# Stick-breaking groups 4 to 6: score matmuls over each head's 64 rows, one split of q for two heads, high parts on ScalarE, the scan's carry read in place

## The chip, the cores and the metric

The kernel runs on one core of one Trainium2 chip. The metric is device time in microseconds (us), the median of several executions. The core has TensorE (PE, with its weight loads as PEld), VectorE (DVE), ScalarE (ACT), GpSimd (POOL) and SyncE (SP, which here issues nearly all DMAs). Each engine works through its own queue in order; engines wait for each other by semaphores.

## The reference

One transformer layer over 2048 tokens of width 1024: a normed projection, differential attention (4 heads) beside stick-breaking attention (8 heads of 64), an output projection and a SwiGLU feed-forward part. What the change touches is the stick-breaking part:

```python
def stick_breaking_attention(q, k, v):
    """A[t,s] = beta_ts * prod_{s<j<t}(1 - beta_tj), s < t."""
    ...
        z = jnp.einsum('bqhd,bkhd->bhqk', qb, k).astype(jnp.float32) * scale
        mask = (k_pos[None, :] < q_pos[:, None])[None, None]
        log_1mb = jnp.where(mask, jax.nn.log_sigmoid(-z), 0.0)
        rem = lax.cumsum(log_1mb, axis=3, reverse=True) - log_1mb
        a = jnp.where(mask, jnp.exp(jax.nn.log_sigmoid(z) + rem), 0.0)
        return jnp.einsum('bhqk,bkhd->bqhd', a.astype(v.dtype), v)
```

Each weight is a sigmoid of the score times the product of (1 - sigmoid) over all later keys up to the query, so the keys are gone through backwards with a running product.

## The kernel before

**Stages.** The first part goes through eight groups: 0 to 3 are the heads of differential attention, 4 to 7 are pairs of stick-breaking heads (a group is m = 0 and m = 1). While group g does its attention, the projections of group g + 1 are made, tile by tile (16 tiles of 128 tokens); `advance` interleaves the two. Then come the output projection and the feed-forward part. The order of instructions on each engine is made by a scheduler that runs a timeline of its own, with the priorities `PRI`; it starts from the order of the program text. `pick` shares work between engines by a running sum of assumed costs in `load`, `note` adds to that sum, and `level` sets it back.

**Precision.** Every f32 operand of a matmul is split in a high and a low f16 part, and three products (high x high, low x high, high x low) are added up in PSUM. The high part is a scaled copy, made on ACT or DVE; the low part is made on DVE from the source and the high part (`split_psum`).

**Projections of groups 4 to 6 ("turned").** `proj_turned` makes q and k already transposed: PSUM tile `pq` has the 64 dimensions of head 0 in partitions 0 to 63 and those of head 1 in partitions 64 to 127, and two tokens' tiles side by side. `turned_out` (L345) takes a pair of tiles, 256 columns, out of PSUM. In `qT` it writes four slots: for each head m a high part and a low part, with `half[:, m]` as the scale, which is 2^-11 on the head's own 64 partitions and 0 on the others. k has one high and one low part for both heads. Group 7 is not turned; it goes through `proj_tile`, `proj_out` and `proj_batch` as the differential groups do.

**Scores.** `score_chunk` (L503) makes the scores of 128 queries against up to 512 keys in one PSUM tile `sc`, of which there are four. For turned groups it multiplies all 128 partitions of a `qT` slot with all 128 of `kT`; the zeros in q take the other head out. At the last chunk of a row of scores one more matmul (L508) adds the mask.

**Stage a** (`stage_a`, L602) goes through a block of up to 1024 keys of one query tile and one head, from the last chunk to the first. `z4` tiles (nine buffers) hold `om` and `be`. ACT makes 1 - beta into `om` and beta into `sc` or `be`. DVE's scan (L621) turns `om` into running products, backwards. Its start value and the neighbour that the multiply needs stand in the column behind the block, `om[:, n]`:

```python
if b == i // 8:
    DVE.memset(om[:, n : n + 1], 8192.0)
else:
    DVE.tensor_copy(om[:, n : n + 1], last[m][:, 0:1])
```

Then beta is multiplied with the products, shifted by one column (L622): on POOL for the second chunk of a turned group (`aside`), else on DVE. `split_t` splits the result (high part on ACT, low part by a subtraction on POOL, L98) and a transposing DMA (L460) brings it to `aT`. A group has 48 such stages.

**Stage b** multiplies `aT` with v on PE (`pv`, L517) some stages later (`lag`); `finish` norms the result.

Of the kernel before, what the change touches and what calls it, by code (L numbers as in the profile page):

```python
# [16 lines left out]
ALU = mybir.AluOpType  # L17
# [4 lines left out]
S, D, P = 2048, 1024, 128  # L22
# [37 lines left out]
def block(tc, a, out):  # L60
# [3 lines left out]
    with top:  # L64
# [8 lines left out]
        def note(e, ns):  # L73
            load[e] += ns * KW[e]
# [38 lines left out]
        def c1(n=1, name="c"):  # L113
            t = cp.tile([P, n], F32, name=nm(name))
            return t
# [10 lines left out]
        mhalf = c1(16, "mh")  # L126
        DVE.memset(mhalf[:], -0.5)

        half = c1(2, "half")
        DVE.memset(half[:], 0.0)  # L130
        for m in range(2):
            DVE.memset(half[64 * m : 64 * m + 64, m : m + 1], 2.0 ** -11)

        def times(o, a_, b_, c=None):
            DVE.tensor_scalar(o[:], a_[:], b_[:], c, op0=ALU.mult, **({} if c is None else {"op1": ALU.mult}))
# [120 lines left out]
        with ExitStack() as ph1:  # L256
# [87 lines left out]
            @pri("po")  # L344
            def turned_out(pq, pv, qT, kT, v, j):  # L345
                two = slice(j - 1, j + 1)
                q2, k2 = (pq[:, 256 * c : 256 * c + 256].rearrange("p (t n) -> p t n", t=2) for c in range(2))
                for m in range(2):
                    ACT.mul(qT[:, m, two, :], q2, half[:, m : m + 1])
                    DVE.scalar_tensor_tensor(qT[:, 2 + m, two, :], q2, half[:, m : m + 1], qT[:, m, two, :], op0=ALU.mult, op1=ALU.subtract)  # L350
                note("A", 800)
                note("D", 800)
                split_psum(kT[:, 0, two, :], kT[:, 1, two, :], k2, 256)
                vv = v[:, two, :].rearrange("p t (h s e) -> p t h s e", h=2, s=2)
                split_psum(vv[:, :, :, 0, :], vv[:, :, :, 1, :], pv[:, :256].rearrange("p (t h e) -> p t h e", t=2, h=2), 256)

            def split_psum(hi, lo, src, n):
                sc = 2.0 ** -11
                if pick(A=0.84 * n + 60, D=1.05 * n + 70) == "A":
                    ACT.mul(hi, src, sc)  # L360
                else:
                    DVE.tensor_scalar(hi, src, sc, None, op0=ALU.mult)
                DVE.scalar_tensor_tensor(lo, src, sc, hi, op0=ALU.mult, op1=ALU.subtract)  # L363
                note("D", 1.05 * n + 70)
# [136 lines left out]

            @pri("sc")
            def score_chunk(G, sc, i, q, m, w, cut=False, turned=False):  # L503
                terms = ((m, 0), (2 + m, 0), (m, 1)) if turned else ((2 + m, m), (m, m))
                for o, (a_, b_) in enumerate(terms):
                    last = PE.matmul(sc[:, : 128 * w].rearrange("p (t n) -> p t n", n=P), lhsT=G["q"][i // 4][:, a_, i % 4, :], rhs=G["k"][q][:, b_, 0:w, :], start=o == 0, stop=o == len(terms) - 1)  # L506
                if cut:
                    last = PE.matmul(sc[:, 128 * w - P : 128 * w], lhsT=idb[:], rhs=tri[:], start=False, stop=True, skip_group_check=True)  # L508
                return last.ins
# [85 lines left out]
            def sb_attn(g, G):  # L595
                last = {}
                front = []
                wide = [0]
                lag = PD + 2 if g < NG - 2 else PD

                @pri("at")
                def stage_a(i, m, b):  # L602
                    L = (i + 1) * 128
                    n = min(1024, L - 1024 * b)
                    be, om = z4(), z4()
                    if b == i // 8:
                        DVE.memset(om[:, n : n + 1], 8192.0)
                    else:
                        DVE.tensor_copy(om[:, n : n + 1], last[m][:, 0:1])
                    last[m] = om  # L610
                    for c in range((n - 1) // 512, -1, -1):
                        lo, hi = 512 * c, min(512 * c + 512, n)
                        w = hi - lo
                        sc = ps.tile([P, 512], F32, tag="sc", bufs=4, name=nm("sc"))
                        front.append(score_chunk(G, sc, i, 2 * b + c, m, w // P, b == i // 8 and hi == n, turned(g)))
                        aside = c == 1 and turned(g)
                        beta = be[:, lo:hi] if aside else sc[:, :w]
                        ACT.activation(om[:, lo:hi], sc[:, :w], AF.Sigmoid, scale=G["nkz"][:])  # L618
                        ACT.activation(beta, sc[:, :w], AF.Sigmoid, scale=G["kz"][:])  # L619
                        ov = om[:, lo:hi][:, ::-1]  # L620
                        DVE.tensor_tensor_scan(ov, ov, sc[:, :w], om[:, hi : hi + 1], op0=ALU.mult, op1=ALU.bypass)  # L621
                        (POOL if aside else DVE).tensor_tensor(be[:, lo:hi], beta, om[:, lo + 1 : hi + 1], ALU.mult)  # L622
# [24 lines left out]
                for i in range(NT):  # L647
                    if i % 4 == 0:
                        level()
                    for b in range(i // 8, -1, -1):  # L650
                        for m in range(2):
                            n, aT = stage_a(i, m, b)
                            pend.append((i, m, b, n, aT))
                            if len(pend) > lag:
                                stage_b(*pend.pop(0))
                            done += n // P + CS
                            yield done / (272 + 48 * CS), (i + 1 if b == 0 and m == 1 else i)
                for u in pend:
                    stage_b(*u)
# [213 lines left out]
        with ExitStack() as ph2:  # L873
# [21 lines left out]
            rows = []  # L895
# [402 lines left out]
```

## Time and profile before

| | |
|---|---|
| median of 3 runs | 2706.24 us (2704.32 to 2712.25) |
| the profiled execution | 2704.82 us |
| its span, first to last instruction | 2702.7 us |
| mean granted TensorE clock | 0.983 |
| busy share PE, DVE, ACT, POOL | 93%, 72%, 50%, 56% |
| scans (L621) | from 602.2 us, the last from 1349.9 us |

The span is what the views of the profile divide. Busy times of PE are too long as a measure of need, since matmuls overlap in the pipeline. The views by stretches give the busy time of each engine between two times; the groups by shape give a line's instructions, their count, busy time, mean length in ns, and the engine's idle time before them with what ended it.

### The profile page before, as it was taken

The numbers are of one execution on the slowest core, as the hardware profiler recorded it, in microseconds if no ns is written. First come the engines' busy times: TensorE is split into PE (matmuls) and PEld (weight loads), VectorE is DVE, ScalarE is ACT, GpSimd is POOL, SyncE is SP. The second block draws the span as 40 slices with busy tenths as digits, with TensorE's granted clock in tenths as the row PEclk, the third lists the DMA queues.
The fourth block names the chain that finished last, engine by engine and source line by source line (L and its number), as shares of the span: only waits on it lengthen the run. The fifth ranks groups of instructions, "written<-read, shape, count | busy, mean of one in ns | idle before, by whom it ended". The sixth has DMA issues, their size and how long they took to land. (4 is left out here: it accounts for less than half of the span.)

```text
span 2702.7 us, 50511 instructions
## 1 busy us (share of the span) xinstructions
PE 2500.8 (93%) x19628; PEld 1502.5 (56%) x19628; DVE 1956.5 (72%) x3711; ACT 1346.4 (50%) x2488; POOL 1516.4 (56%) x1097
## 2 busy tenths in 40 slices
PE   7998989898988989889998999999999999999999
PEld 4655556577776776567784444444444444444444
DVE  6888879899989989877856777778685543433434
ACT  4665656567978878665735534345352112111121
POOL 2577767767767767546655565565564332322322
PEclk9999999999999999999999999999999999999999
DMA  7777687769989989987995566565749744635532
GB/s 230 201 166 180 143 200 173 178 151 178 196 176 185 178 169 209 206 200 211 222 335 204 210 236 220 198 234 190 253 171 338 293 158 160 234 132 184 201 111 94
DMA packets 619584, 534.40 MB, mean 198 GB/s; under 512 B 480640, under 2 KB 548224, under 8 KB 609104
## 3 DMA queue, kind: packets, MB, share of 16 engines
q1 hardware_dynamic: 617520, 529.09, 69.8%
q8 instruction: 154, 2.52, 0.4%
q0 software_dynamic: 512, 1.36, 0.2%
q10 hardware_dynamic: 1312, 0.72, 0.1%
q14 instruction: 86, 0.70, 0.1%
HBM read 261.08 MB, written 147.32 MB: 151 GB/s over the span
## 5 line engine op out<-in xcount | busy, mean ns | idle before, releaser
L98 POOL TENSOR_TENSOR s<-z,s 128x1024 f16<-128x1024 f32 (+7 forms) x288 | 471.9, 1648 | 140.9 <-ACT s L89 116.3
L506 PE MATMUL sc<-kT,qT 128*128 128x512 f16 (+3 forms) x1520 | 381.6, 353 | 53.5 <-DVE z L622 19.0
L1104 PE MATMUL pd<-wd,act 128*128 128x512 f16 x1764 | 391.8, 379 | 8.1 <-DVE cu L1038 7.1
L621 DVE TENSOR_TENSOR_SCAN z<-z,sc 128x512 f32<-128x512 f32 (+3 forms) x320 | 352.8, 1112 | 56.7 <-ACT sc L619 34.9
L325 PE MATMUL pj<-w,xt 128*128 128x384 f16 x1920 | 353.1, 332 | 17.2 <-ACT raw L374 5.9
L1004 PEld LDWEIGHTS <-wg 128*128 128x128 f16 x1848 | 181.5, 98 | 226.1 <-issue 12.4
L1004 PEld LDWEIGHTS <-wu 128*128 128x128 f16 x1848 | 181.5, 98 | 220.2 <-issue 7.1
L517 PE MATMUL yp<-v,aT 128*128 128x64 f16 (+1 forms) x4896 | 269.1, 204 | 37.3 <-DMA aT<-s 36.2
L517 PEld LDWEIGHTS <-aT 128*128 128x128 f16 x4896 | 236.9, 99 | 115.4 <-DMA aT<-s 47.7
L98 POOL TENSOR_TENSOR act<-cg,act 128x512 f16<-128x512 f32 x109 | 150.6, 1392 | 262.5 <-ACT act L1063 262.5
L1104 PEld LDWEIGHTS <-act 128*128 128x128 f16 x1764 | 172.6, 98 | 216.6 <-issue 10.1
L325 PEld LDWEIGHTS <-xt 128*128 128x128 f16 x1920 | 187.5, 99 | 146.9 <-issue 23.3
L89 ACT CAST s<-z 128x128 f16<-128x128 f32 (+7 forms) x215 | 173.1, 810 | 135.8 <-DMA aT<-s 41.0
L98 POOL TENSOR_TENSOR stages<-stages 128x512 f32<-128x512 f32 x97 | 171.6, 1769 | 119.1 <-DVE wg L220 41.3
L618 ACT ACTIVATE z<-sc,c 128x512 f32<-128x512 f32 (+3 forms) x320 | 210.6, 663 | 25.1 <-PE sc L506 12.5
L98 POOL TENSOR_TENSOR hs<-hs,cu 128x512 f32<-128x512 f32 x102 | 132.5, 1307 | 158.1 <-DVE hs L1110 58.0
L506 PEld LDWEIGHTS <-qT 128*128 128x128 f16 x1520 | 128.2, 99 | 121.4 <-issue 23.5
L1063 ACT CAST act<-cg 128x512 f16<-128x512 f32 x126 | 76.8, 616 | 237.5 <-DVE cg L1069 199.4
L831 PE MATMUL po<-wo,mt 128*128 128x256 f16 x1536 | 182.5, 279 | 12.2 <-DVE xf L834 8.4
L1110 DVE SCALAR_TENSOR_TENSOR hs<-pd,c,hs 128x512 f32<-128x512 f32 x144 | 106.5, 748 | 116.3 <-PE pd L1104 112.2
L341 PE MATMUL pj<-xt,w 128*128 128x128 f16 x2304 | 176.9, 222 | 6.2 <-DVE v L363 5.2
L1004 PE MATMUL pm<-X,wu 128*128 128x512 f16 x792 | 179.3, 379 | 1.8 <-ACT cg L1049 1.7
(255 smaller groups left out, 4803.5 us busy)
## 6 DMA issues: line engine op xcount, KB each, us to landing
xt<-xs SPq DMA_DIRECT2D x112, 512.0 KB, 4.3
hs<-hd SPq DMA_DIRECT2D x72, 512.0 KB, 4.4
hd<-hs SPq DMA_DIRECT2D x56, 512.0 KB, 5.4
split<-wg SPq DMA_DIRECT2D x11, 1792.0 KB, 6.9
split<-wu SPq DMA_DIRECT2D x11, 1792.0 KB, 6.7
split<-wd SPq DMA_DIRECT2D x11, 1792.0 KB, 6.8
wg<-split SPq DMA_DIRECT2D x11, 1792.0 KB, 7.3
wd<-split SPq DMA_DIRECT2D x11, 1792.0 KB, 8.7
```

Of the source, the lines that this page charges most:

```text
L89: ACT.copy(dst, src)
L98: (DVE if e == "D" else POOL).tensor_tensor(dst, a_, b_, op)
L325: PE.matmul(pj[:, :384], lhsT=xv[:, xi, kt, :], rhs=G["w"][:, wi, kt, :], start=n == 0, stop=n == 23)
L341: PE.matmul(o, lhsT=x_ if c == 2 else w_, rhs=w_ if c == 2 else x_, start=n == 0, stop=n == 23)
L506: last = PE.matmul(sc[:, : 128 * w].rearrange("p (t n) -> p t n", n=P), lhsT=G["q"][i // 4][:, a_, i % 4, :], rhs=G["k"][q][:, b_, 0:w, :] ...
L517: PE.matmul(yp[:, y0 : y0 + wd], lhsT=aT[:, a_, :], rhs=v[:, v_ : v_ + wd], start=start and j == 0 and q == 0, stop=stop and j == nb - 1 a ...
L618: ACT.activation(om[:, lo:hi], sc[:, :w], AF.Sigmoid, scale=G["nkz"][:])
L621: DVE.tensor_tensor_scan(ov, ov, sc[:, :w], om[:, hi : hi + 1], op0=ALU.mult, op1=ALU.bypass)
L831: PE.matmul(po[:, sl], lhsT=mt[:, kt, P * xi : P * xi + P], rhs=wos[2 * h + n][wi][:, kt, :], start=q == 0, stop=q == 23)
L1004: PE.matmul(ps_[:].rearrange("p (t n) -> p t n", n=P), lhsT=wv[:, wo, wi, 128 * kt : 128 * kt + 128], rhs=X[xo][:, :, xi, kt, :], start=st ...
L1104: PE.matmul(po[:], lhsT=act[:, ao, xi, 128 * j : 128 * j + 128], rhs=W["d"][:, wo, wi, :], start=start and u == 0 and q == 0, stop=u == nu ...
L1110: DVE.scalar_tensor_tensor(dst, po[:], kd[:], src, op0=ALU.mult, op1=ALU.add)
```

## The change

Four things change, all of them in the stick-breaking groups.

- `turned_out` makes one high and one low part of q for both heads, in slots 0 and 1 of `qT`, by `split_psum`; the tile `half` is gone, and so are the two `note` lines. All three high parts (q, k, v) of the turned groups are made on ACT (`he="A"`); the low parts stay on DVE.
- `score_chunk` takes for turned groups the 64 partitions of head m from q and from k, instead of all 128. The number of matmuls and their columns stay, as do the other matmuls.
- The column behind the block, `om[:, n]`, is written by POOL, not by DVE, in all four stick-breaking groups.
- The scan's start value is read from where it comes from: a constant tile `full`, the first column of the block done before (`last[m]`), or the first column of the chunk done before. The multiply at L622 still reads the column.

```diff
-        half = c1(2, "half")
-        DVE.memset(half[:], 0.0)
-        for m in range(2):
-            DVE.memset(half[64 * m : 64 * m + 64, m : m + 1], 2.0 ** -11)
+        full = c1(1, "full")
+        DVE.memset(full[:], 8192.0)
...
             def turned_out(pq, pv, qT, kT, v, j):
...
-                for m in range(2):
-                    ACT.mul(qT[:, m, two, :], q2, half[:, m : m + 1])
-                    DVE.scalar_tensor_tensor(qT[:, 2 + m, two, :], q2, half[:, m : m + 1], qT[:, m, two, :], op0=ALU.mult, op1=ALU.subtract)
-                note("A", 800)
-                note("D", 800)
-                split_psum(kT[:, 0, two, :], kT[:, 1, two, :], k2, 256)
+                split_psum(qT[:, 0, two, :], qT[:, 1, two, :], q2, 256, "A")
+                split_psum(kT[:, 0, two, :], kT[:, 1, two, :], k2, 256, "A")
                 vv = v[:, two, :].rearrange("p t (h s e) -> p t h s e", h=2, s=2)
-                split_psum(vv[:, :, :, 0, :], vv[:, :, :, 1, :], pv[:, :256].rearrange(...), 256)
+                split_psum(vv[:, :, :, 0, :], vv[:, :, :, 1, :], pv[:, :256].rearrange(...), 256, "A")
-            def split_psum(hi, lo, src, n):
+            def split_psum(hi, lo, src, n, he="AD"):
                 sc = 2.0 ** -11
-                if pick(A=0.84 * n + 60, D=1.05 * n + 70) == "A":
+                cost = {"A": 0.84 * n + 60, "D": 1.05 * n + 70}
+                if pick(**{e: cost[e] for e in he}) == "A":
...
             def score_chunk(G, sc, i, q, m, w, cut=False, turned=False):
-                terms = ((m, 0), (2 + m, 0), (m, 1)) if turned else ((2 + m, m), (m, m))
+                rows = slice(64 * m, 64 * m + 64) if turned else slice(0, P)
+                terms = ((0, 0), (1, 0), (0, 1)) if turned else ((2 + m, m), (m, m))
                 for o, (a_, b_) in enumerate(terms):
-                    ... lhsT=G["q"][i // 4][:, a_, i % 4, :], rhs=G["k"][q][:, b_, 0:w, :] ...
+                    ... lhsT=G["q"][i // 4][rows, a_, i % 4, :], rhs=G["k"][q][rows, b_, 0:w, :] ...
...
                     if b == i // 8:
-                        DVE.memset(om[:, n : n + 1], 8192.0)
+                        begin = full[:]
+                        POOL.memset(om[:, n : n + 1], 8192.0)
                     else:
-                        DVE.tensor_copy(om[:, n : n + 1], last[m][:, 0:1])
+                        begin = last[m][:, 0:1]
+                        POOL.tensor_scalar(om[:, n : n + 1], begin, 1.0, 0.0, op0=ALU.mult, op1=ALU.add)
...
-                        DVE.tensor_tensor_scan(ov, ov, sc[:, :w], om[:, hi : hi + 1], op0=ALU.mult, op1=ALU.bypass)
+                        DVE.tensor_tensor_scan(ov, ov, sc[:, :w], begin, op0=ALU.mult, op1=ALU.bypass)
+                        begin = om[:, lo : lo + 1]
```

More of the change, by code (lines that the diff above doesn't have):

```diff
@@ L503, in score_chunk @@
             def score_chunk(G, sc, i, q, m, w, cut=False, turned=False):
-                terms = ((m, 0), (2 + m, 0), (m, 1)) if turned else ((2 + m, m), (m, m))
+                rows = slice(64 * m, 64 * m + 64) if turned else slice(0, P)
+                terms = ((0, 0), (1, 0), (0, 1)) if turned else ((2 + m, m), (m, m))
                 for o, (a_, b_) in enumerate(terms):
-                    last = PE.matmul(sc[:, : 128 * w].rearrange("p (t n) -> p t n", n=P), lhsT=G["q"][i // 4][:, a_, i % 4, :], rhs=G["k"][q][:, b_, 0:w, :], start=o == 0, stop=o == len(terms) - 1)
+                    last = PE.matmul(sc[:, : 128 * w].rearrange("p (t n) -> p t n", n=P), lhsT=G["q"][i // 4][rows, a_, i % 4, :], rhs=G["k"][q][rows, b_, 0:w, :], start=o == 0, stop=o == len(terms) - 1)
                 if cut:
```

2 lines of the change are left out of this document (1 added, 1 removed).

## The prediction

> **What bounds the kernel now.** I read the page first for the span, then the view by stretches for the stick-breaking part, then the groups by shape inside that part, then the waits of the score matmuls.
>
> ```profile
> span 2702.7 us, 50511 instructions
> PE 2500.8 (93%) x19628; PEld 1502.5 (56%) x19628; DVE 1956.5 (72%) x3711; ACT 1346.4 (50%) x2488; POOL 1516.4 (56%) x1097
> ```
>
> The average says "TensorE", but the change touches one part only: groups 4 to 7, which last from the first scan at 602 us to the last at 1351. The scans come 80 to a group; the 1st, 81st, 161st and 241st begin at 602, 762, 921 and 1092 us, and these are the stretches (busy us of PE, PEld, DVE, ACT, POOL; granted clock; DMA share; GB/s).
>
> ```profile
> core 0: us, PE busy (x) PEld busy (x) DVE busy (x) ACT busy (x) POOL busy (x), PEclk, DMA share, GB/s
> 602.00:762.00 160.00, 145.90 (x2227) 118.37 (x2224) 148.18 (x256) 138.93 (x259) 123.26 (x92) 0.98 0.94 185
> 762.00:921.00 159.00, 142.26 (x2260) 114.85 (x2258) 144.99 (x252) 132.73 (x242) 117.21 (x89) 1.00 0.95 185
> 921.00:1092.00 171.00, 152.31 (x2071) 114.66 (x2066) 150.26 (x266) 131.37 (x238) 116.96 (x89) 0.97 0.92 187
> 1092.00:1351.00 259.00, 228.12 (x2367) 178.09 (x2366) 204.68 (x356) 165.78 (x305) 146.37 (x101) 0.96 0.86 209
> ```
>
> Groups 4 to 6 take 490 us. In them DVE works 148.18 + 144.99 + 150.26 = 443 us, ACT 403, POOL 357. PE's 440 us overstate it, since a matmul's record holds its pipeline as well. What PE really needs is the count of each shape times the distance between starts when nothing is waited for. The distances come from an undisturbed piece of the timeline (start, length, how many):
>
> ```profile
> 840.62 0.82 PE L506 MATMUL sc<-kT,qT 128*128 128x512 f16 x3 [0.62 <-DVE z L622]
> 841.27 0.57 PE L517 MATMUL yp<-v,aT 128*128 128x64 f16 x14
> 841.68 0.64 PE L488 MATMUL yp<-id,y 128*128 128x128 f32 x4
> 842.15 0.46 PE L517 MATMUL yp<-v,aT 128*128 128x64 f16 x10
> 851.24 2.24 PE L341 MATMUL pj<-xt,w 128*128 128x128 f16 x37
> ```
>
> Three score matmuls over 512 columns fill 841.27 - 840.62 = 0.65 us, 0.217 each; fourteen over 64 columns 0.41 us, 0.029 each; thirty-seven over 128 columns 2.24 us less one pipeline of 0.2, 0.056 each. It goes by columns. The counts from 602 to 1092 us:
>
> ```profile
> L341 PE MATMUL pj<-xt,w 128*128 128x128 f16 x2016 | 154.1, 222 | 6.1 <-DVE v L363 5.2 <-POOL z L622 0.9
> L506 PE MATMUL sc<-kT,qT 128*128 128x512 f16 x504 | 138.8, 386 | 21.7 <-DVE z L622 10.7 <-DVE z L609 4.0 <-DVE z L621 3.4
> L517 PE MATMUL yp<-v,aT 128*128 128x64 f16 x2352 | 105.0, 194 | 10.1 <-DMA aT<-s 10.0
> L341 PE MATMUL pj<-w,xt 128*128 128x128 f16 x1008 | 90.0, 219 | 0.0
> L325 PE MATMUL pj<-w,xt 128*128 128x384 f16 x168 | 29.1, 326 | 0.3 <-DVE v L363 0.3
> L508 PE MATMUL sc<-tri,idb 128*128 128x128 bf16 x97 | 21.3, 221 | 0.0
> L506 PE MATMUL sc<-kT,qT 128*128 128x384 f16 x72 | 16.3, 326 | 1.5 <-DVE z L607 1.4
> L506 PE MATMUL sc<-kT,qT 128*128 128x256 f16 x74 | 12.7, 280 | 1.4 <-DVE z L622 1.0 <-DVE z L621 0.3
> L517 PE MATMUL yp<-v,aT 128*128 128x128 f16 x130 | 9.5, 224 | 0.4 <-DMA aT<-s 0.4
> L506 PE MATMUL sc<-kT,qT 128*128 128x128 f16 x70 | 8.6, 223 | 2.1 <-DVE z L607 1.0 <-DVE z L621 0.4 <-DVE z L622 0.3
> ```
>
> At 0.217, 0.165, 0.110, 0.056 and 0.029 us for 512, 384, 256, 128 and 64 columns: projections 3024 x 0.056 + 168 x 0.165 = 197; scores 504 x 0.217 + 72 x 0.165 + 74 x 0.110 + 70 x 0.056 = 133; values 2352 x 0.029 + 130 x 0.056 = 75; cuts 97 x 0.056 = 5; with some 60 small ones at about 0.12 (7 us) PE needs 418 us of 490. So DVE is the tallest (443, 47 us idle), PE second (418, 72 idle), ACT third. And PE, when it stands at a score matmul, mostly waits for DVE (us, times, 602 to 1092):
>
> ```profile
>   DVE z L622: 25.7, 33
>   DVE z L607: 9.3, 16
>   DVE z L609: 8.8, 14
>   DVE z L621: 4.0, 11
> ```
>
> 48 of PE's 72 idle us are these: a score buffer that DVE gives back late.
>
> **DVE's part of the change (a gain).** Rows of 540 to 1092 us for the splits, of the whole run for the carry column:
>
> ```profile
> L350 DVE SCALAR_TENSOR_TENSOR qT<-pj,half,qT 128x256 f16<-128x256 f32 x48 | 22.7, 473 | 2.4 <-ACT qT L349 2.3
> L362 DVE TENSOR_SCALAR kT<-pj 128x256 f16<-128x256 f32 x20 | 8.2, 412 | 0.0
> L362 DVE TENSOR_SCALAR v<-pj 128x256 f16<-128x256 f32 x15 | 6.1, 408 | 0.6 <-PE pj L341 0.5
> L609 DVE COPY z<-z 128x1 f32<-128x1 f32 x64 | 8.2, 143 | 0.0
> L607 DVE MEMSET z<- 128x1 f32 x128 | 7.2, 59 | 0.3 <-POOL s L98 0.3
> ```
>
> Half of the low q parts go: 24 x 0.473 = 11.3 us. All high k and v parts leave DVE: 8.2 + 6.1 = 14.3. The carry column leaves it: 15.4, three quarters of it in groups 4 to 6 (11.6), a quarter in group 7 (3.8). In groups 4 to 6 that is 37 us, a little of it before 602: say 35, and DVE falls from 443 to 408.
>
> **ACT's part (even).**
>
> ```profile
> L349 ACT ACTIVATE qT<-pj,half 128x256 f16<-128x256 f32 x48 | 24.6, 513 | 21.6 <-PE pj L341 15.2 <-DVE qT L350 6.3
> L360 ACT ACTIVATE v<-pj 128x256 f16<-128x256 f32 x9 | 4.0, 442 | 1.6 <-PE pj L341 1.6
> L360 ACT ACTIVATE kT<-pj 128x256 f16<-128x256 f32 x4 | 1.5, 386 | 0.6 <-DVE qT L350 0.6
> ```
>
> 48 q parts at 0.513 (24.6 us) become 24 at about 0.386 (9.3), and 20 k parts and 15 v parts come over at 0.386 and 0.442 (14.4): 24.6 out, 23.7 in. ACT stays at 402.
>
> **POOL's part (a cost beside the path).** The carry column's 128 fills and 64 copies go to POOL. The nearest rows are its one-column fills at the start and its smallest arithmetic, over four columns (ns: least, median, most):
>
> ```profile
> L1284 POOL MEMSET const-float32-0.0<- x1: 100/100/100, 0.2 to 0.2; 128x1 f32 x1
> L484 POOL TENSOR_SCALAR yrs<-yrs x16: 233/242/1212, 136.7 to 631.4; 128x4 f32<-128x4 f32 x16
> ```
>
> 96 x 0.10 + 48 x 0.24 = 21 us in groups 4 to 6: POOL goes from 357 to 379, still the lowest. The scan now reads its carry from the old place and waits for no column, but the multiply behind the first chunk still reads the column, so it now waits for POOL.
>
> **PE's part (a cost).** The number of score matmuls and their columns stays. What changes is that they work on 64 rows of the array, among projections, values and cuts on 128. The kernel before has one such case, the bias matmuls on 32 rows, and the last of them lies at full clock:
>
> ```profile
> 32.97 0.49 PE L325 MATMUL pj<-w,xt 128*128 128x384 f16 x2
> 33.38 0.91 PE L703 MATMUL bt<-z,z 32*128 32x384 f32 x2
> 34.22 0.66 PE L325 MATMUL pj<-w,xt 128*128 128x384 f16 x3
> ```
>
> The second L325 begins at 32.97 + 0.165 = 33.13 and is followed at 33.38 instead of 33.30: 0.09 us lost on the way in. The two L703 take until 34.22, 0.84 us, where two f32 matmuls over 384 columns need 2 x 3 x 0.12 = 0.70 (the four L488 above: 0.47 for 4 x 128): 0.14 more, shared by an uncovered f32 weight load and the way out. So a visit to fewer rows costs 0.23 here, of which the f16 scores, with their shorter load, should pay about 0.09 in, 0.09 out and 0.02 of load. The control is the timeline above: going from L517 to f32 L488 and back, all on 128 rows, costs nothing (14 x 0.029 ends at 841.68; 4 x 0.12 at 842.15). So it is the number of rows that costs, not the type or the line.
>
> The Trainium skill, TensorEngine Tiling (Array Packing), Key Properties, says that changing the tiling mode drains TensorE, while changing the tile within a mode does not. It gives no time for it; the rows above agree, and by that rule every visit of the new score matmuls pays.
>
> In the changed kernel's built order the 720 score matmuls of groups 4 to 6 stand in 230 separate visits, 194 of them the three matmuls of one chunk. So PE pays 230 x 0.20 = 46 us, and needs 418 + 46 = 464 of the 490. A bound below zero is not excluded by this alone: if 64 rows behaved unlike 32, it would be 0; the upper bound is 230 x 0.27 = 62, with the row's whole surplus and rounding.
>
> **The sum.** PE 464, DVE 408, ACT 402, POOL 379: the relief on DVE is real, but PE takes its place as the tallest. If PE keeps only the idle time that is not DVE's late score buffers, 72 - 48 = 24 us, the stretch is 488 (2 shorter); if it keeps as much as DVE, the tallest of before, had, 47 us, it is 511 (21 longer). Between them I take the middle, 499.5, 10 us longer. Group 7 uses 128-row scores as before; it loses 3.8 us of DVE work where DVE has 259 - 205 = 54 us idle: nothing, within 4 us. What lies behind needs all groups' outputs (the out-projection, then the feed-forward part), so a gain or loss here moves the end by as much. The profiled execution took 2704.82 us, 2.1 beyond its span; the median shown is 2706.24. I put the 10 us on the median: 2716.
>
> **Rivals.**
> *Switching is cheap at 64 rows.* Then PE stays at 418, and the tallest is 418 with DVE's 47 idle us: 465, 25 shorter, 2681. For it: the row is of 32 rows and f32, and was seen at full clock once. Against: its loss on the way in cannot come from the f32 load. It decides when a visit costs under (443 - 418) / 230 = 0.11 us.
> *The carry column comes late from POOL.* In 16 of the 48 stages of each group 4 to 6 the multiply that reads it is DVE's, and in the built order 99 of the 192 columns stand straight behind one of POOL's subtractions:
>
> ```profile
> L98 POOL TENSOR_TENSOR s<-z,s 128x1024 f16<-128x1024 f32 x120 | 266.1, 2222 | 56.0 <-ACT s L89 45.0 <-issue 6.0 <-DVE x L98 2.6
> ```
>
> DVE is in order, so the scans and multiplies queued behind it stand too, and PE stands for their score buffers. If all 48 waited for a whole subtraction, DVE would get 48 x 2.22 = 107 more, 515, and with 24 idle 539: 49 longer, 2755. It decides once (464 - 408) / 2.22 = 25 of the 48 wait so long. Against it: the fills wait only for an old buffer, and POOL is idle for a quarter of the time.
> *Two heads at once.* In 13 visits matmuls of rows 0 to 63 and of 64 to 127 stand together; if they overlapped wholly, the shorter sides, 12672 columns in all, would be saved: 12672 / 512 x 0.217 = 5 us, and the end 2711. The Trainium skill, TensorE: Matmul & The Clock Gate, Part 3, says that matmuls in different row groups run concurrently; no row of before shows it.
>
> **How the numbers follow.** About 0.3%, 8 us, is what a measurement of this kernel can tell from no change. Forecast 0.57: from 2 shorter to 37 longer (62 us of switching, 480 + 47 = 527), of which 0.40 lie beyond 8 us longer, 0.14 within, 0.03 before it, for an order that changed otherwise. Cheap switching 0.28, faster. Late column 0.10, slower. Two heads at once 0.05, within. So faster 0.31, same 0.19, slower 0.50. The range goes from 2678, a little beyond cheap switching, to 2743, the forecast's upper end; forecast alone 2704 to 2743.
>
> **What would show it.** In the profile after, starts around a 64-row score group should stand about 0.09 us further apart than its columns on both sides; DVE's busy time in groups 4 to 6 should be near 408 and its idle time up by 30 or more; PE's waits for DVE z at the score matmuls should shrink from 48 us to under 20, and the waits for L607 and L609 vanish. POOL's fills should take 0.1 us. I am wrong if 64-row visits cost no time, or if DVE's multiplies wait for POOL by tens of us.

## The result, and the profile after

The changed kernel takes 2745.34 us in the median (2738.05 to 2751.05, 6 runs), the kernel before 2708.12 us beside it (2703.47 to 2712.25): a ratio of 1.0134, interval 1.0116 to 1.0151, 37 us slower. The forecast was 2716, from 2678 to 2743: the direction was right, the size was not, and the time lies 2 us beyond the range. The profiled execution took 2751.05 us. The first lines of its page:

```profile
span 2749.3 us, 50586 instructions
PE 2558.7 (93%) x19628; PEld 1505.7 (55%) x19628; DVE 1929.3 (70%) x3458; ACT 1349.3 (49%) x2500; POOL 1531.4 (56%) x1288
```

The span is 46.6 us longer. Where this lies is seen from the stretches between the 1st, 81st, 161st and 241st scan and the last one (busy us of PE, PEld, DVE, ACT, POOL; granted clock; DMA share; GB/s):

```profile
605.40:774.80 169.40, 162.88 (x2210) 116.59 (x2207) 140.13 (x189) 139.96 (x261) 126.88 (x140) 0.94 0.89 177
774.80:942.50 167.70, 152.79 (x2044) 108.25 (x2043) 133.71 (x179) 133.46 (x246) 119.72 (x135) 0.91 0.84 169
942.50:1134.20 191.70, 178.44 (x2316) 124.18 (x2316) 146.76 (x205) 134.99 (x247) 125.67 (x140) 0.93 0.84 175
1134.20:1392.00 257.80, 231.24 (x2348) 179.14 (x2344) 199.90 (x307) 163.89 (x304) 147.07 (x145) 0.95 0.83 208
```

Groups 4 to 6 take 528.8 us instead of 490, 39 of the 46.6. The scans begin 3.2 us later, group 7 is 1 shorter, and what follows the last scan is 5.8 longer. In these three stretches DVE works 420.6 us (443.4 before), ACT 408.4 (403), POOL 372.3 (357). So VectorE is busy 23 us less and stands still 108 us instead of 47. And the granted clock, 0.98, 1.00 and 0.97 before, is 0.94, 0.91 and 0.93.

The cost of a visit to 64 rows can be read from the timeline (start, length, how many):

```profile
700.42 0.46 PE L513 MATMUL yp<-v,aT 128*128 128x64 f16 x10
700.81 0.82 PE L502 MATMUL sc<-kT,qT 64*128 64x512 f16 x3
701.56 0.58 PE L513 MATMUL yp<-v,aT 128*128 128x64 f16 x14
```

Ten matmuls of 64 columns need 0.29 us, so the scores could start at 700.71 and start at 700.81; three of 512 columns need 0.65 and the next group starts 0.75 later: 0.10 on the way in and 0.10 on the way out. Over all 227 visits of groups 4 to 6 the medians are 0.096 and 0.092 us.

The idle time before the score matmuls, by what ended it (us, times), from the view of their line, groups 4 to 6. It is the view in which the prediction read its 48 us, and it adds the idle time of two engines, that of the weight loads (PEld) and that of the matmuls (PE):

```profile
  ACT kT L355: 11.9, 7
  issue: 9.5, 31
  DVE qT L358: 8.7, 5
  DVE z L621: 6.7, 9
  ACT qT L355: 2.1, 2
```

In this count the 48 us of late score buffers are down to 7 (L621), and the waits for L607 and L609 are gone, as forecast. The matmuls alone waited less; first before, then after, groups 4 to 6 (us, times, longest):

```profile
PE sc L506 <- DVE z L622: 12.1, 17, 1.6
PE sc L506 <- DVE z L607: 5.1, 8, 1.0
PE sc L506 <- DVE z L609: 4.0, 7, 1.6
PE sc L506 <- DVE z L621: 4.0, 11, 0.9
```

```profile
PE sc L502 <- ACT kT L355: 11.9, 7, 3.5
PE sc L502 <- DVE z L621: 3.1, 5, 1.1
```

So 25 us before and 3 after are time in which the matmuls stood for a score buffer. The other 23 of the 48 are the weight loads', 17 of them in the very moments in which the matmuls stood. In place of these waits the matmuls now wait 12 us for the new k parts (kT), and weight loads 11 us for the new q parts (qT). The other side of the loop is what VectorE waits for; first before, then after, groups 4 to 6:

```profile
DVE z L621 <- ACT z L619: 12.1, 8, 4.0
DVE z L621 <- ACT sc L619: 10.8, 17, 2.5
```

```profile
DVE z L619 <- ACT sc L617: 42.6, 38, 4.4
DVE z L619 <- ACT z L617: 19.2, 15, 3.1
DVE qT L358 <- ACT qT L355: 7.8, 4, 3.7
DVE kT L358 <- ACT kT L355: 3.9, 5, 1.5
```

The scan (L621 before, L619 after) waits 62 us for ScalarE's sigmoids instead of 23. Where VectorE was relieved, it now waits for the step ahead of it.

To compare runs below, PE's time between the 1st and the 241st scan is divided from the trace's records in four parts: its columns at the distances of the prediction ("need"); what these columns take longer where the granted clock is half; the surplus at a change between 64 and 128 rows; and the rest, in which it stands. The parts exceed the stretch by 1 to 6 us, since some matmuls overlap or follow each other closer than these distances (in the paired run, which is left out here, much more).

| groups 4 to 6, us | length | need | half clock | visits | stands | DVE, ACT, POOL busy |
|---|---|---|---|---|---|---|
| before | 489.8 | 415.8 | 7.6 | 0 | 68.7 | 443, 403, 357 |
| after | 528.7 | 412.4 | 33.0 | 44.3 | 44.9 | 421, 408, 372 |
| rows_only | 520.6 | 415.1 | 23.1 | 45.5 | 39.3 | 445, 406, 355 |
| rows_pinned | 501.8 | 415.5 | 11.6 | 45.2 | 33.4 | 444, 404, 357 |
| after_wide | 514.6 | 411.8 | 18.0 | 0 | 86.0 | 419, 406, 372 |
| after_pinned | 503.1 | 415.0 | 11.3 | 45.4 | 33.9 | 416, 405, 369 |
| high_pinned | 516.7 | 415.7 | 11.5 | 0 | 91.9 | 433, 414, 357 |
| no_high_pinned | 501.0 | 415.3 | 14.0 | 45.4 | 29.1 | 428, 395, 369 |

### The profile page after: what moved, and what is told of

It is laid out like the page before. It is cut to its first block, busy times and chain, and to the rows that moved or that the text cites. A ratio compares the mean times of both kernels' runs of the same rounds, so it can differ in the third digit from the quotient of the medians.

```text
span 2749.3 us, 50586 instructions
## 1 busy us (share of the span) xinstructions
PE 2558.7 (93%) x19628; PEld 1505.7 (55%) x19628; DVE 1929.3 (70%) x3458; ACT 1349.3 (49%) x2500; POOL 1531.4 (56%) x1288
## 5 line engine op out<-in xcount | busy, mean ns | idle before, releaser
L502 PE MATMUL sc<-kT,qT 128*128 128x512 f16 (+7 forms) x1520 | 383.6, 357 | 33.1 <-ACT kT L355 11.9
L323 PE MATMUL pj<-w,xt 128*128 128x384 f16 x1920 | 363.4, 338 | 19.3 <-ACT raw L369 5.8
L513 PE MATMUL yp<-v,aT 128*128 128x64 f16 (+1 forms) x4896 | 284.9, 206 | 38.9 <-DMA aT<-s 38.5
L89 ACT CAST s<-z 128x384 f16<-128x384 f32 (+7 forms) x216 | 172.1, 803 | 134.9 <-DMA aT<-s 45.4
L339 PE MATMUL pj<-xt,w 128*128 128x128 f16 x2304 | 189.7, 229 | 3.9 <-DVE v L358 3.4
L619 DVE TENSOR_TENSOR_SCAN z<-z,sc 128x512 f32<-128x512 f32 x128 | 163.2, 1275 | 25.6 <-ACT sc L617 18.1
L1003 PE MATMUL pm<-X,wg 128*128 128x512 f16 x792 | 180.4, 381 | 0.0
```

The costliest lines, as they stand in the source:

```text
L89: ACT.copy(dst, src)
L323: PE.matmul(pj[:, :384], lhsT=xv[:, xi, kt, :], rhs=G["w"][:, wi, kt, :], start=n == 0, stop=n == 23)
L339: PE.matmul(o, lhsT=x_ if c == 2 else w_, rhs=w_ if c == 2 else x_, start=n == 0, stop=n == 23)
L513: PE.matmul(yp[:, y0 : y0 + wd], lhsT=aT[:, a_, :], rhs=v[:, v_ : v_ + wd], start=start and j == 0 and q == 0, stop=stop and j == nb - 1 a ...
L619: DVE.tensor_tensor_scan(ov, ov, sc[:, :w], begin, op0=ALU.mult, op1=ALU.bypass)
L1003: PE.matmul(ps_[:].rearrange("p (t n) -> p t n", n=P), lhsT=wv[:, wo, wi, 128 * kt : 128 * kt + 128], rhs=X[xo][:, :, xi, kt, :], start=st ...
```

## The experiments

**What 64 rows do to TensorE (rows_clock, one execution).** The layer is left out. TensorE alone goes through stretches of matmuls, each behind some 9 to 14 us in which it stands: 160 of 512 columns on 128 rows, on 64 and on 32 rows; 320 that alternate between rows 0 to 63 and 64 to 127; 160 on 128 rows with half of the weights zero; and four mixes like the kernel's.

```python
mm(w, j, 0, 0, r1)                       # 160 times, r1 = 128, 64 or 32
mm(w, j // 2, m, 64 * m, 64 * m + 64)    # 320 times, m = j % 2
```

> A kernel of its own that leaves the whole layer out and only measures: nine stretches of f16 matmuls, each behind about 12 us in which PE has nothing to do, so that each begins at half clock. In order: 160 matmuls over 512 columns on 128 rows; 160 on 64 rows; 320 alternating between rows 0 to 63 and 64 to 127, each half in a bank of its own; 160 on 128 rows with weights that are zero in one half; 160 on 32 rows; then cycles of three score matmuls (512 columns) with twelve of 128 columns and twelve of 64 columns on 128 rows: the scores on 128 rows, on 64 rows, on 128 rows with one 16-column matmul on 64 rows between them; and on 64 rows with twice as much of the 128-row work. Theory 1 (what grants the clock counts few rows as little work): the first stretch is back at full clock after one or two steps of 3.4 us; the second stays at half clock to its end (0.43 us a matmul, 68 us) or far longer than the first; the cycle with 64-row scores is held at half clock for tens of us, the one with the 16-column visits is not. Theory 2 (the idle time at the changes of mode holds the clock down): the second stretch, which has no change, recovers like the first, and both cycles with visits are held alike. Either way a visit should cost about 0.19 us at full clock. If rows 0 to 63 and 64 to 127 overlap, the third stretch takes about 0.11 us a matmul, else 0.217.

Its timeline, the first five stretches in the order 128 rows, 64 rows, alternating, half zero, 32 rows:

```profile
13.80 36.00 PE L43 MATMUL b<-k,w 128*128 128x512 f16 x160 [13.80 <-DVE w L37]
58.60 68.44 PE L43 MATMUL b<-k,w 64*128 64x512 f16 x160 [8.79 <-DVE w L37]
135.84 36.42 PE L43 MATMUL b<-k,w 64*128 64x512 f16 x320 [8.79 <-DVE w L37]
182.23 37.11 PE L43 MATMUL b<-k,w 128*128 128x512 f16 x160 [9.97 <-DVE w L39]
228.13 68.44 PE L43 MATMUL b<-k,w 32*128 32x512 f16 x160 [8.79 <-DVE w L37]
```

Every stretch begins at half clock, with 0.427 us between starts. On 128 rows the distance falls to 0.216 after 2.7 us. On 64 or on 32 rows it stays 0.427 for all 68 us: work on few rows does not bring the clock back. Zero weights do no harm, and the alternating halves recover after 3.5 us; their 320 matmuls take 0.114 us each, so two heads do run at once. The mix with 64-row scores stayed at half clock for 92 us; the same mix with 128 rows for 4.6, the one with 16-column visits for 3.1, and 64-row scores among twice as much 128-row work for 5.2. So the first theory held in this run: the share of the work on few rows held the clock down, not the changes. The Trainium skill, TensorE: Matmul & The Clock Gate, Part 1, has the clock return after about one busy window of 3.4 us; the 128-row rows agree, the 64-row rows do not, and here the measurement decides.

The kernel shows it too. Six windows of 3.4 us in group 4 (busy us as above; the clock stands third from the right), and for four of them what of PE is score matmuls:

```profile
646.70:650.10 3.40, 3.02 (x19) 1.92 (x18) 2.54 (x4) 3.40 (x8) 1.99 (x3) 0.50 0.90 219
650.10:653.50 3.40, 3.40 (x25) 2.09 (x23) 3.33 (x15) 0.88 (x3) 1.79 (x2) 0.50 0.65 148
653.50:656.90 3.40, 3.40 (x29) 2.19 (x28) 3.40 (x4) 2.53 (x5) 3.40 (x4) 0.50 0.03 7
656.90:660.30 3.40, 3.40 (x26) 2.09 (x25) 3.40 (x4) 1.45 (x3) 3.40 (x3) 0.50 0.02 3
660.30:663.80 3.50, 3.50 (x48) 3.21 (x46) 3.50 (x4) 1.93 (x5) 3.50 (x2) 0.51 0.69 128
663.80:667.20 3.40, 3.40 (x69) 3.19 (x67) 0.62 (x2) 0.00 (x0) 2.31 (x3) 1.00 0.31 69
```

```profile
650.10:653.50 3.40, 1.46 (x3) 0.00 (x0) 0.00 (x0) 0.50 0.65 148
653.50:656.90 3.40, 1.46 (x3) 0.00 (x0) 0.00 (x0) 0.50 0.03 7
656.90:660.30 3.40, 1.46 (x3) 0.00 (x0) 0.00 (x0) 0.50 0.02 3
660.30:663.80 3.50, 0.50 (x3) 0.00 (x0) 0.00 (x0) 0.51 0.69 128
```

In this piece PE is busy through three whole windows and the clock stays at half as long as 1.46 of the 3.40 us are on 64 rows; behind the window with 0.50 it comes back. From 600 to 1100 us the kernel before has five periods of half clock, all of one window; after has ten, up to 17 us long. after_wide, which has the order of after but all scores on 128 rows, has ten as well, none over 6.8 us: in this order the half clock comes without the 64 rows, and they draw it out.

**One part at a time, order made anew.** Each of these is the kernel before with one part of the change; the scheduler writes the order again.

rows_only has the 64-row slices alone:

```diff
-... lhsT=G["q"][i // 4][:, a_, i % 4, :], rhs=G["k"][q][:, b_, 0:w, :] ...
+... lhsT=G["q"][i // 4][rows, a_, i % 4, :], rhs=G["k"][q][rows, b_, 0:w, :] ...
```

> The kernel before, with only the score matmuls of groups 4 to 6 cut to the head's 64 rows; four q slots, DVE's high parts and the carry column stay as they were. Theories 1 and 2 (the loss is PE's): as slow as the full change or slower, since DVE's relief is missing: 2740 to 2770 us, some 45 us of changes of mode and 25 us or more of half clock over before in groups 4 to 6. Theory 3 (the loss comes from the other parts, high parts that are late from ACT or a carry that is late from POOL): within 10 us of before, 2708.

2731.48 us, ratio 1.008 (1.0059 to 1.010): between what the theories had, so the 64 rows cost something, but not all.

switch_only leaves the scores at 128 rows and adds to each chunk one matmul of 16 columns on 64 rows whose products are zeros:

```diff
+                    if turned and o == 2:
+                        rows = slice(64 - 64 * m, 128 - 64 * m)
+                        PE.matmul(sc[:, :16], lhsT=G["q"][i // 4][rows, m, i % 4, :], rhs=G["k"][q][rows, 0, 0, 0:16], ...)
```

> The kernel before, with one matmul more in each chunk of scores of groups 4 to 6, on the other head's 64 rows, where q's slot is zero, over 16 columns: it adds zero, and makes 240 visits to 64 rows with next to no work on them. Theory 1: the visits cost 240 x 0.2 = 48 us of PE time, part of it taken from PE's idle time, and the half-clock time in groups 4 to 6 stays near before's 8 us lost: 2710 to 2735. Theory 2: the half clock comes as with the full change, 25 us and more, 2740 or above.

2729.17 us, 1.007 (1.0053 to 1.0086): 240 visits with hardly any columns cost nearly what the 64-row scores cost. The visits take 47.5 us of PE, and half clock 7.3 as before; both as theory 1 had it.

full_rows has all of the change that the 128 rows allow: high parts on ACT, carry column on POOL, scan in place, but q split twice.

> The kernel before, with the high parts of k and v on ACT, the carry column on POOL and the scan's carry read in place, but with scores on 128 rows and so with four q slots. Theories 1 and 2: faster than before, DVE loses about 27 us of its 443 in groups 4 to 6 and PE nothing: 2680 to 2700. Theory 3: slower than 2708.

2717.12 us, 1.0031 (1.0019 to 1.0044). DVE is busy 425 us instead of 443, and the kernel is slower all the same, as theory 3 had it.

high_only moves the high parts of k and v to ACT (`split_psum(..., "A")`), carry_only moves the carry column to POOL and lets the scan read in place.

> The kernel before, with only the high parts of k and v of groups 4 to 6 always on ACT. If ACT, which scans wait for, is what full_rows lost to (scans' waits for ACT 23 us before, 43 in full_rows): 4 to 12 us slower, 2713 to 2721. If not: 2700 to 2709, since DVE loses 14 us of work.

> The kernel before, with only the carry column on POOL and the scan's carry read in place. full_rows, which has this and the high parts on ACT, was 8 us slower than before although DVE does less. If POOL's copies cost it (they wait for the block before, 8.7 us in full_rows, with subtractions, transposes and ACT's casts queued behind them): this alone is 5 to 12 us slower, 2714 to 2721, and high_only is at before or faster. If not: at before or up to 8 us faster.

high_only takes 2740.19 us, 1.0123 (1.0093 to 1.0154); carry_only 2727.31, 1.0074 (1.005 to 1.0098), both slower than any of the expectations. Alone, either costs more than the two together (full_rows). Costs that add up in this way are not costs of the work that was moved, and the next question was the order.

**The order of before kept.** The same program is built twice: once as before, to take its order on every engine, and once with the edit, where the instructions that both have are tied to that order:

```python
for places in order.values():            # of the kernel before, engine by engine
    for a, b in zip(places, places[1:]):
        tc.add_manual_dep(ins[b], ins[a].name, queued, reason="order")
```

rows_pinned is rows_only in the order of before; full_in_rows_order is the reverse, the kernel before in the order of rows_only; tiny_pinned is switch_only in the order of before.

> rows_only with every engine's instructions in exactly the order of the kernel before: each is queued behind the one that stood before it there, which adds no wait. Only the rows of the 720 score matmuls differ from before. Theory P (PE pays: 237 visits at 0.19 us, and the half clock that is held on): as rows_only, 2722 to 2738, with some 45 us of changes and 15 to 25 us of half clock in groups 4 to 6. Theory O (any edit makes the scheduler write a new order, and the order of before is a good one): within 8 us of before, 2698 to 2716.

> The other half: the kernel before, its work unchanged, in exactly the order that rows_only has. Theory P: within 8 us of before. Theory O: as slow as rows_only, 2722 to 2738, with no change of mode in it.

> switch_only in exactly the order of before, each of the 240 small 64-row matmuls behind its chunk's second score matmul. Theory P: 240 x 0.19 = 46 us of PE time, of which PE's idle time gives back about 25: 2722 to 2735, half clock as before (under 12 us lost in groups 4 to 6). Theory O: within 8 us of before. If this is as slow as rows_pinned, the half clock costs nothing of its own; if rows_pinned is 8 us or more above it, that is its price.

rows_pinned: 2719.84 us, 1.004 (1.0021 to 1.006). full_in_rows_order: 2715.61, 1.0036 (1.0018 to 1.0055). tiny_pinned: 2719.99, 1.0044 (1.0025 to 1.0063). So the 64-row scores cost 10 us, the bare visits cost the same 10, and the other half of rows_only's price is its order, which costs about that much without a single 64-row score: 10 us by the ratio, 6 by the medians. For rows_pinned and tiny_pinned neither theory had this size; full_in_rows_order came out within the 8 us of theory P, short of the 2722 of theory O. In rows_pinned VectorE works as much as before, and yet the matmuls wait only 7 us for its score buffers (3.9, 1.9 and 1.2) instead of 25: the time that the visits take on TensorE is in part time that it had stood there anyway.

**Parts taken out of the full change, order made anew.** paired lets the chunks of both heads alternate in one visit (139 visits instead of 230), dve_carry gives the carry column back to DVE, and after_wide keeps the exact order of the changed kernel but multiplies all 128 rows (which leaves out the separation of the two heads).

```diff
-                        POOL.tensor_scalar(om[:, n : n + 1], begin, 1.0, 0.0, op0=ALU.mult, op1=ALU.add)
+                        DVE.tensor_copy(om[:, n : n + 1], begin)
```

> The full change, with both heads' chunks of groups 4 to 6 made together: six score matmuls in turn on rows 64 to 127 and 0 to 63, each head in its own buffer, queued behind each other; two fills of eight columns first, so that both buffers are free. 107 of 139 visits hold all six. If half the rows being idle is what holds the clock down, both halves at work take the hold away: half-clock loss in groups 4 to 6 back from 33 to about 10 us; 139 visits cost 27 us instead of 44; and with the overlap that rows_clock showed (0.114 us a matmul) the scores need about 75 us instead of 133. PE then needs some 390 us and DVE (421) or ACT (408) is the tallest: 2680 to 2710. If taking two score buffers at once starves ACT instead, it stays above 2725 with PE idle at the scores.

> The full change with the carry column back on DVE; the scan still reads its carry in place. If POOL's late copies matter: 5 to 12 us faster than the full change, 2733 to 2741. If not: 2743 to 2752, since DVE has 12 us more to do in groups 4 to 6 but is not the tallest.

> The full change, in exactly its own order, but with all 128 rows in the score matmuls: it leaves out the separation of the two heads, whose scores are added up. The instructions, their order and columns are those of the full change; only the array's mode never changes. The distance to the full change (2745) is what PE's mode costs there, and the distance to before (2708) what moved work and order cost. Theory P: 2700 to 2718. Theory O: 2730 to 2745.

paired: 2736.20 us, 1.0119 (1.009 to 1.0148). dve_carry: 2737.30, 1.0112 (1.0085 to 1.014). after_wide: 2738.19, 1.0111 (1.009 to 1.0133). None gives back more than 9 of the 37 us by the medians, or 6 by the ratios. paired missed its 2680 to 2710 by far: its granted clock in groups 4 to 6, 0.94, 0.92 and 0.92, is no better than the change's, and its matmuls wait 53 us for two score buffers at once. dve_carry's median lies in the range written down for late copies of POOL, but its interval overlaps that of the change. after_wide is the telling one: without any 64-row matmul 30 us of the loss are still there, and the 64 rows cost some 6 us in this order (1.0134 against 1.0111), which is not clear of the noise. Its stretches of groups 4 to 6, and its largest wait on PE:

```profile
604.80:765.40 160.60, 143.67 (x2217) 117.38 (x2215) 139.63 (x190) 139.51 (x263) 126.04 (x139) 0.98 0.96 187
765.40:931.10 165.70, 137.94 (x2048) 110.71 (x2044) 133.32 (x178) 132.37 (x244) 120.25 (x136) 0.93 0.85 171
931.10:1119.40 188.30, 160.40 (x2299) 122.98 (x2296) 146.26 (x205) 133.76 (x247) 125.55 (x140) 0.96 0.83 175
```

```profile
PE sc L503 <- ACT kT L356: 22.5, 7, 5.8
```

PE has 86 us to spare in 514.6, DVE 95: in this order nothing is full, and the engines wait for each other.

**Moved work or new order.** Four edits in the order of before: the high parts, the carry column, both, and the whole change with its 64-row scores and single split of q. In all four builds the scheduler itself places the carry column, the high parts of k and v that VectorE made before, and the second head's split of q, moved or not; everything else is tied to the order of before.

> Only the high parts of k and v of groups 4 to 6 go to ScalarE; every instruction that the kernel before has too stands in the order that it had there on its engine, and only the moved ones are placed by the scheduler. The same edit with a free order took 2740.19 us. Theory A (the order written anew costs the time): 2703 to 2713, and TensorE's waits for DVE v at the projections (19 us with the free order) fall back to under 10. Theory B (the moved work costs it, ScalarE's high parts come late in a queue that goes in order): 2725 or more, with the waits for ACT kT at the scores at 10 us or more.

> Only the carry column goes to GpSimd and the scan reads its carry in place; all shared instructions in the order of before. With a free order it took 2727.31 us. Theory A (order): 2703 to 2713, DVE's busy time in groups 4 to 6 lower by about 10. Theory B (the column comes late from GpSimd): 2718 or more, with DVE's multiplies waiting for GpSimd by over 8 us.

> Both moves together, scores on all 128 rows, q split twice as before, all shared instructions in the order of before. With a free order it took 2717.12 us. Theory A (order): 2695 to 2710, since DVE has about 25 us less to do in the same order. Theory B (moved work): 2715 or more.

> The whole change, 64-row scores and one split of q among it, with all shared instructions in the order of before. In its own order the change takes 2745. Theory A (order): 2712 to 2722, the 10 us of the 64-row scores alone in that order, or less by some of DVE's relief. Theory B (moved work): 2735 or more, as with its own order. Between them both have a share, by the distance from each end.

high_pinned: 2731.68 us, 1.009 (1.0071 to 1.011). carry_pinned: 2711.01, 1.0007 (0.9995 to 1.0018). full_pinned: 2739.35, 1.0115 (1.0097 to 1.0133). after_pinned: 2728.09, 1.007 (1.0053 to 1.0086). Theory A holds for the carry column (so the freely placed instructions cost nothing by themselves), theory B for the high parts and for both moves together, and the whole change lies between. Theory B's sign did not come: the score matmuls wait 3 us for ACT's kT in high_pinned, not 10. What the high parts cost stands in VectorE's waits there:

```profile
DVE kT L378 <- ACT kT L375: 23.3, 13, 4.5
DVE v L378 <- ACT v L375: 9.1, 9, 2.9
```

Before, DVE made a high part itself and went on with the low part behind it; there no such wait reached 1 us. Now it waits 32 us for ACT, and its own busy time falls by 11 (443.3 to 432.6). In after_pinned 18.7 us of this waiting are left (nearly all for v), and the scans wait 38 us for the sigmoids. In the changed kernel, with its own order, VectorE waits 12 us for high parts (7.8 for q, 3.9 for k, 0.7 for v).

**The change without the moved high parts.** no_high is the change with k and v shared between ACT and DVE as before, in an order made anew; no_high_pinned is the same in the order of before.

```diff
-                split_psum(kT[:, 0, two, :], kT[:, 1, two, :], k2, 256, "A")
+                split_psum(kT[:, 0, two, :], kT[:, 1, two, :], k2, 256)
```

> The full change, but the high parts of k and v are shared between ScalarE and VectorE by pick as before; the order is made anew by the scheduler. Theory H (the moved high parts cost most of what is beyond the 64-row scores): 2745 less about 20, so 2718 to 2730. Theory O (any order made anew costs about that, whatever is moved): 2735 or more.

> The full change without the move of the high parts of k and v: 64-row scores, one split of q, carry column on GpSimd, scan in place, every shared instruction in the order of before. With the high parts moved too it took 2728.09 us. Theory H: the 64-row scores' 10 us alone are left, 2710 to 2722, and VectorE's waits for ACT v and ACT kT (19 us) are gone. Theory O would put it at 2728 or near it, since the order is the same.

no_high: 2732.75 us, 1.009 (1.0073 to 1.0107), 12 less than the full change but slower than theory H had it. no_high_pinned: 2723.30, 1.006 (1.0045 to 1.0075), a little above the 2710 to 2722 of theory H; the waits for ACT's v and kT are gone as it said (1.2 us left), but its interval overlaps that of after_pinned. Neither theory alone carries it. All pairs together, as surplus over the kernel before (ratio less 1):

| edit | order of before | order made anew |
|---|---|---|
| 64-row scores | 0.40% | 0.80% |
| 16-column visits | 0.44% | 0.70% |
| carry column and scan in place | 0.07% | 0.74% |
| high parts | 0.90% | 1.23% |
| high parts and carry column | 1.15% | 0.31% |
| change without high parts | 0.60% | 0.90% |
| whole change | 0.70% | 1.34% |

In six of seven rows the order made anew costs 0.26 to 0.67% more (7 to 18 us); in one it is cheaper by 0.84% (23 us). There VectorE waits 37 us for ACT's k and v parts with the order of before (full_pinned) and 3 with the new one (full_rows). The smallest of the differences, 0.26%, is not clear of the noise. So the 37 us are, as far as the runs tell: 10 for the visits to 64 rows, 9 for the other edits in an unchanged order (of which the moved high parts are 3 and not certain, the intervals overlap), and 17 for the order, to which what `pick` shares out anew is counted. These parts hold for taking the steps in this way and not for each alone: the high parts cost 24 us as the only edit (high_pinned) and 3 beside the others, the 64 rows 10 us in the order of before and 6 in the changed kernel's own. That half clock is held longer goes with the order: with that of before it is 11 to 14 us in the four such runs of the first table, with 64 rows or without; with new orders it is 18 without 64 rows (after_wide), and 23 and 33 with them. Which of the scheduler's many exchanges costs the 17 us stays open. No version was faster than the kernel before; carry_pinned can't be told from it.

## Why the prediction was wrong, step by step

*What bounds the kernel.* That PE waits for VectorE's score buffers was read rightly, and these waits went. Their size was not: the 48 us count the idle time of matmuls and of weight loads, and the matmuls alone stood 25. Counted from start to start, as the 72 us of idle time are, that is about 33, an estimate with 0.17 us of pipeline (0.386 less 0.217) for each of the 43 waits. That this time would then be had was wrong as well: it went into the steps ahead in the same loop.

*DVE's part.* The removed rows left as forecast: the records of VectorE in groups 4 to 6, added up, fall by 37 us (485.6 to 448.4). But 443 is the time in which at least one of them is at work, and neighbours overlap in the profile, by 42 us before and 28 after. So DVE came to 421 instead of 408: rows that lay in part under others were taken off in full, and the relief was 23 us, not 35.

*ACT's and POOL's parts.* These lines of the profile after, groups 4 to 6, answer to the estimates:

```profile
L355 ACT ACTIVATE kT<-pj 128x256 f16<-128x256 f32 x21 | 8.8, 420 | 3.1 <-DVE qT L358 3.1
L355 ACT ACTIVATE qT<-pj 128x256 f16<-128x256 f32 x21 | 8.5, 405 | 10.6 <-PE pj L339 10.6
L607 POOL TENSOR_SCALAR z<-z 128x1 f32<-128x1 f32 x48 | 11.8, 255 | 14.1 <-DVE z L619 14.1
L604 POOL MEMSET z<- 128x1 f32 x97 | 9.0, 100 | 2.1 <-DVE z L621 1.9
```

A q part takes 405 ns (386 forecast), a fill 100 (100), a copy 255 (240); POOL's new work is 20.8 us (21). But "even" counted busy time alone. It left out that a low part on DVE now waits for a high part from another engine: 12 us in the changed kernel, 32 in high_pinned.

*PE's part.* Right: 227 visits (230) at 0.19 us (0.20), 44 us (46); need and visits are 457 us (464). The prediction cited two rules from the Trainium skill. The drain at a change of mode (TensorEngine Tiling (Array Packing), Key Properties) agrees with the runs in that every change costs time, 0.096 and 0.092 us; that it is a drain no run shows. Two row groups at once (TensorE: Matmul & The Clock Gate, Part 3) agrees: 0.114 us a matmul.

*The sum.* This is the step that failed. It put PE's idle time, all that is neither need nor visits, at 24 to 47 us instead of 72, since DVE's relief would take the 48 us of waiting away. It stayed at 72 (528.7 - 412.4 - 44.3); half clock, which is within it, rose from 8 to 33 of these, and a new wait of 12 us for k parts is in the rest. Three things were wrong in it. The 48 us were 25 to 33, so that even by its own rule the stretch would have begun at about 503 instead of 488. The relief does not give the time back: with the order kept, idle time falls to 41 us in rows_pinned and 43 in after_pinned, with 444 and 416 us of DVE work and stretches of 501.8 and 503.1, so the visits fill TensorE's waits and the relief is worth nothing that can be told; carry_pinned, with 8 us less of DVE work, is not faster either. The prediction did not name what is late next, the sigmoids behind the scores, for which the scans wait 23 us before and 62 after. And it took the order to stay as good as it was; with a new order idle time is back at 72. The forecast's 10 us are what rows_pinned measures, but that is luck: it is the middle of two ends, of which the lower takes off waits counted twice, for a relief that gives nothing. "An order that changed otherwise" was given 0.03, as a gain; it was the largest term, as a loss.

*The rivals.* Cheap switching: refuted, by rows_pinned and tiny_pinned. The late carry column: not shown. DVE's multiplies wait 2 us for POOL's columns and carry_pinned costs nothing; dve_carry gains 8 us by the medians, with intervals that overlap, so a few us are not excluded. Two heads at once: the overlap is real, but paired with its 139 visits is not surely faster than the change (1.009 to 1.0148 against 1.0116 to 1.0151).

*Group 7 and behind.* Group 7 changed by 1 us, as forecast; the start of the scans and what lies behind them, 9 us together in the profiled executions, were not in the sum.

## What to carry to other kernels

When several engines in a loop are 80 to 90% busy, ask of a relief which step of the loop is late next, and count a hand-over to another engine as a wait, not only as busy time moved: as the only edit, the moved high parts took 11 us off VectorE and made it wait 32. Look which engine's idle time a view adds up: weight loads and matmuls together gave 48 us where the matmuls stood 25. A cost that falls into idle time and a relief of the same idle time can't both be counted. Where a scheduler writes the order anew after every edit, the order is a term of its own, here 7 to 18 us of loss in six pairs and 23 of gain in one; keep the old order once to see what the edit itself costs. Fewer rows in a matmul among others with more rows cost 0.19 us of TensorE's time a visit here, of which about a quarter came out as time of the kernel (10 of 45 us).

## What the runs showed of the hardware that was not expected

- After a pause, matmuls on 64 or 32 rows do not bring TensorE back to full clock: 0.427 us for 512 columns through all 68 us, where 128 rows take 0.216 after 2.7 us. Two alternating halves bring it back after 3.5 us, and 128 rows with half of the weights zero do so too (160 matmuls in 37.11 us).
- Two matmuls on different halves of the rows overlap wholly: 320 of 512 columns in 36.42 us, 0.114 each.
- A change between 64 and 128 rows costs 0.096 us in and 0.092 us out, whether the visit has 16 columns or three times 512 (0.096 and 0.103 in switch_only).
